# Feed-forward blocks 2 to 4 of a diffusion trunk: four tile pairs with a late 1/rms, eighteen with a normed operand

## The chip, the core and the metric

The kernel runs on one core of a Trainium2 chip. TensorE (PE) multiplies a stationary tile of 128 by 128 (PEld loads it) with a moving operand and writes into PSUM; VectorE (DVE) and ScalarE (ACT) work on tiles of 128 partitions; GpSimd (POOL) and SyncE (SP) issue transfers here. The metric is the device time of one execution in microseconds (us), the median of three.

## The reference

Two layers of a diffusion trunk over 256 latent tokens and 256 context tokens, width 1024. Each layer is a half-step feed-forward, token mixing, and a second half-step feed-forward. The context is needed only up to the first layer's mixing, so the first feed-forward block has 512 columns and the other three have 256. What the change touches is this:

```
def rms_norm(x, g):
    y = xf * lax.rsqrt(jnp.mean(xf * xf, axis=-1, keepdims=True) + EPS)
    return y * g
def modulate(x, g, shift, scale):
    return rms_norm(x, g) * (1 + scale) + shift
def swiglu(h, w13, w2):
    a, b = jnp.split(h @ w13, 2, axis=-1)        # 1024 -> 2 x 2816
    return (jax.nn.silu(a) * b) @ w2
def half_ffn(x, g, shift, scale, gate, w13, w2):
    return x + 0.5 * gate * swiglu(modulate(x, g, shift, scale), w13, w2)
```

## The kernel before

Activations lie with features on the partitions and tokens along the free dimension: X holds 8 parts (k = 0 to 7) of 128 features. Every product is made from split numbers: a float32 operand becomes a rounded high half (a CAST on ACT, L153) and the remainder (a subtraction on DVE, L154), and `mm3` issues three matmuls per part of the contraction: low weight by high operand (L148), high by high (L149), high weight by low operand (L150).

A feed-forward block first makes 22 pairs of tiles, f = 0 to 21 (one tile for `a`, one for `b`). A pair takes 2 tiles by 8 parts by 3 matmuls, 48 in all, of w13. `load_w` brings the pair's weights (raw, 2 buffers, issued by SP) and splits them in two halves of 1024 columns into whi and wlo (3 buffers each). `glu` then makes silu(a) * b and splits it into HH and HL. After pairs 0 to 10, and again after 11 to 21, eight products with w2 (33 matmuls each) are added to X.

In blocks 2 to 4 (`ffn` called with fi = 1, 2, 3 and n = T = 256) the norm is deferred. While the products before them still run, `prep_raw` writes the operand gs * x into AH and AL, columns 0 to 255, and `prep_shift` writes the shift into columns 256 and 257. The product is 258 columns wide, so that its last columns hold the shift's share. 1/rms is known later: `rstd` (L172 to L174: a matmul, a square root, a reciprocal into rb) is called after the first pair's products. `glu` multiplies each product with rb and adds the shift's column. The same columns 258 to 513 of AH and AL hold other operands in the mixers, where `prep_full` writes a fully normed operand for part of `mixer_c` (L192 to L194), and where `out_proj` reads its operand OH and OL, 256 columns wide.

Each engine works through its own list of instructions in order and waits on semaphores; a scheduler sets the order in each list when the kernel is built. In the trace block 2 runs its pairs from 504 us, block 3 from 695 us, block 4 from 959 us.

Of the kernel before, what the change touches and what calls it, by code (L numbers as in the profile page):

```python
# [29 lines left out]
# columns of the parameter table and of the constant table  # L30
# [5 lines left out]
def trunk(ctx: ExitStack, tc: tile.TileContext, I, out):  # L36
# [20 lines left out]
    # streams: 0 latent in layer 0, 1 context in layer 0, 2 latent in layer 1  # L57
# [26 lines left out]
    def finish_mod(layer, j, n=1, ks=slice(0, NK)):  # L84
        """add the bias to rows j .. j + n - 1; a scale becomes g * (1 + scale), the gates of
        half steps are halved"""
        st = slice(2, 3) if layer else slice(0, 2 if j < 5 else 1)
        ns, nk = st.stop - st.start, ks.stop - ks.start
        m = mod.rearrange("p s (j k) -> p s j k", k=NK)[:, st, j:j + n, ks]
        b = par[:, C_BMOD + layer * NMOD:C_BMOD + (layer + 1) * NMOD]  # L90
        b = b.rearrange("p (j k) -> p j k", k=NK)[:, j:j + n, ks].unsqueeze(1)
        V.tensor_tensor(out=m, in0=m, in1=b.broadcast_to([P, ns, n, nk]), op=ALU.add)
        sub, kind = (j + n - 1) // 3, (j + n - 1) % 3
        last = m[:, :, n - 1]
        if kind == 1:
            g0 = C_NG + (layer * 3 + sub) * NK
            g = par[:, g0 + ks.start:g0 + ks.stop].unsqueeze(1).broadcast_to([P, ns, nk])
            V.scalar_tensor_tensor(out=gs[:, st, sub, ks], in0=last, scalar=1.0, in1=g,
                                   op0=ALU.add, op1=ALU.mult)
        if kind == 2:  # L100
            V.tensor_scalar(gate[:, st, sub, ks], last, 1.0 if j == 5 else 0.5, None, ALU.mult)
# [4 lines left out]
    def run_mods(share):  # L106
        """take up modulation jobs as VectorE has room for them"""
        room[0] += share
        while mod_jobs:
            layer, i = mod_jobs[0]  # L110
            cost = 2 if layer == 0 and i < 40 else 1
            if room[0] < cost:
                return
            room[0] -= cost
            mod_jobs.pop(0)
            use_mod(layer, i, load_mod(layer, i, nc.gpsimd), tc.keep_in_program_order)
            if i % 8 == 7:
                finish_mod(layer, i // 8)
# [15 lines left out]
    def in_tiles(hi, lo, mhs, offs, w, late=False):  # L134
        """output tiles mhs of a pair, on the operand columns from each of offs; late: the
        products with the last part of the operand come last"""
# [30 lines left out]
    def rstd():  # L167
        """1 / rms of the rows whose squares acc holds; the users call it after their first products"""
# [13 lines left out]
    def prep_raw(k, off, xs, g):  # L182
        """operand parts of gs * x; the factor 1/rms follows after the product"""
# [5 lines left out]
    def prep_full(k, off, xs, r, g, sh):  # L189
        """operand parts of x / rms * gs + shift"""  # L190
        h = tmp.tile([P, T], F32, name="hn", bufs=2)
        V.tensor_tensor(out=h, in0=xs, in1=r, op=ALU.mult)  # L192
        S.activation(out=h, in_=h, func=AF.Identity, scale=g, bias=sh)
        split(AH[:, k, off:off + T], AL[:, k, off:off + T], h)  # L194

# [19 lines left out]
    def ffn(fi, layer, sub, n, mods, after, started=()):  # L215
        """n = T: latent only; n = 2T: latent | context share the products"""
        defer = n == T
        with tc.tile_pool(name=f"ffn{fi}", bufs=1) as fp:
            HH = fp.tile([P, NH, 2 * T], F32R, name="HH")
            HL = fp.tile([P, NH, 2 * T], F32R, name="HL")  # L220
            for half in range(2):
                hc = half * T if n == T else 0
                for fl in range(NH):
# [3 lines left out]
                    else:  # L227
# [3 lines left out]
                        ps = in_tiles(hi, lo, (0, 1), (0,), T + 2 if defer else n, late=f == 0)  # L231
# [45 lines left out]
    def out_proj(src, srcs, layer, after, loaded=()):  # L277
        """x += gate * (srcs @ w)"""
# [19 lines left out]
    def mixer_a(after):  # L298
        with tc.tile_pool(name="mixa", bufs=1) as mp:
# [12 lines left out]
            # keys and values of one key group, zero on the other group's rows / columns  # L312
# [9 lines left out]
            # the context's half of X is free from here on  # L322
# [11 lines left out]
            def proj(pair, mh, dst, ps=None, part=0):  # L334
                """dst = projected tile / rms, returns the shift's column"""
# [8 lines left out]
            def rotate(z):  # L344
                """rotary embedding; both elements of a pair have the same angle"""
# [98 lines left out]
            # unit u: head t of key group 0 or t + 4 of group 1, one block of 128 queries  # L444
# [177 lines left out]
    # ---- the first tiles, contraction outermost: each part of the modulation is used as it comes  # L622
    def start():
        ng = 4
        order = (0, 5, 1, 6, 2, 7, 3, 4)
        with tc.tile_pool(name="start", bufs=1) as sp:
# [14 lines left out]
            # brings the square root's table in while the squares are still to come  # L641
            S.activation(out=rb[:, 0:1], in_=cT[:, 0, 0:1], func=AF.Sqrt, scale=0.0, bias=epsb)
            # the vectors, on every partition
# [31 lines left out]
            def by_rows():  # L675
                """shift and scale of the last two parts, with the vectors as stationary operand"""
# [67 lines left out]
def _pack(x, c, ctx, c_ctx, w_mod, b_mod, norm_g, ffn_w13, ffn_w2, w_in_a, qk_norm_g, pool_w,  # L744
# [37 lines left out]
    # constants of the shapes alone  # L782
# [40 lines left out]
```

## Time and profile before

| | us |
|---|---|
| runs, median (lowest to highest) | 1156.89 (1154.97 to 1157.5) |
| span of the profiled execution | 1153.2 |
| PE busy in the span | 1143.4 (99%) |
| PEld busy | 1050.5 (91%) |
| DVE busy | 877.1 (76%) |
| ACT busy | 527.6 (46%) |

The page gives no time for the profiled execution beside its span. The span lies 3.7 us under the median of the runs; that is the time around it that the profile does not show. A matmul's own duration in the profile overlaps the next ones, so what a matmul costs is read from start to start.

### The profile page before, as it was taken

The numbers are of one execution on the slowest core, as the hardware profiler recorded it, in microseconds if no ns is written. First come the engines' busy times: TensorE is split into PE (matmuls) and PEld (weight loads), VectorE is DVE, ScalarE is ACT, GpSimd is POOL, SyncE is SP. The second block draws the span as 40 slices with busy tenths as digits, with TensorE's granted clock in tenths as the row PEclk, the third lists the DMA queues.
The fourth block names the chain that finished last, engine by engine and source line by source line (L and its number), as shares of the span: only waits on it lengthen the run. The fifth ranks groups of instructions, "written<-read, shape, count | busy, mean of one in ns | idle before, by whom it ended". The sixth has DMA issues, their size and how long they took to land.

```text
span 1153.2 us, 19338 instructions
## 1 busy us (share of the span) xinstructions
PE 1143.4 (99%) x7752; PEld 1050.5 (91%) x7752; DVE 877.1 (76%) x1614; ACT 527.6 (46%) x834; POOL 71.7 (6%) x148
## 2 busy tenths in 40 slices
PE   8999999999999999999999999999999999999998
PEld 4888888888888898999999999999999899999998
DVE  5968787878789988778778888756767788766763
ACT  5552212232223367665334456434445867434442
POOL 0000110212122200000010000000000000000000
PEclk9999999999999999999999999999999999999999
DMA  8835556788898930446587655446547535546543
GB/s 328 306 138 173 179 191 223 290 305 322 290 305 290 319 136 11 182 166 223 179 311 261 228 204 204 176 151 224 182 147 243 179 141 206 186 152 213 190 147 117
DMA packets 52410, 242.74 MB, mean 211 GB/s; under 512 B 5600, under 2 KB 11488, under 8 KB 38880
## 3 DMA queue, kind: packets, MB, share of 16 engines
q1 hardware_dynamic: 33888, 174.39, 42.6%
q0 software_dynamic: 18432, 67.12, 17.2%
q8 instruction: 61, 1.00, 0.4%
q14 instruction: 29, 0.24, 0.1%
HBM read 240.44 MB, written 1.05 MB: 209 GB/s over the span
## 4 chain that ended last, share of the span: by engine, by line
PE 98%; DVE 1%; ACT 1%; DMA 0%; issue 0%; SPq 0%
PE ps L150 31%; PE ps L148 31%; PE ps L149 31%; PE ps L473 1%; PE ps L681 1%; PE ps L602 1%; PE ps L603 1%; PE ps L601 1%; PE ps L664 1%; PE ps L649 0%; DVE wlo L154 0%; PE ps L172 0%; PE ps L350 0%; DMA ident<-in_ident 0%; PE ps L351 0%; DVE st L455 0%
## 5 line engine op out<-in xcount | busy, mean ns | idle before, releaser
L148 PE MATMUL ps<-AH,wlo 128*128 128x258 f32 (+2 forms) x1664 | 507.2, 305 | 0.3 <-ACT AH L153 0.3
L149 PE MATMUL ps<-AH,whi 128*128 128x258 f32 (+2 forms) x1664 | 506.6, 305 | 0.0
L150 PE MATMUL ps<-AL,whi 128*128 128x258 f32 (+2 forms) x1664 | 505.4, 305 | 0.0
L153 ACT CAST whi<-raw 128x1024 fp32r<-128x1024 f32 (+2 forms) x354 | 313.7, 921 | 362.4 <-PE ps L150 261.8
L154 DVE TENSOR_TENSOR wlo<-raw,whi 128x1024 fp32r<-128x1024 f32 (+2 forms) x354 | 367.6, 1064 | 54.8 <-ACT whi L153 53.7
L148 PEld LDWEIGHTS ps<-AH,wlo 128*128 128x128 f32 x1664 | 316.3, 190 | 15.3 <-PE ps L150 0.5
L149 PEld LDWEIGHTS ps<-AH,whi 128*128 128x128 f32 x1664 | 314.3, 189 | 14.8 <-issue 0.5
L150 PEld LDWEIGHTS ps<-AL,whi 128*128 128x128 f32 x1664 | 313.4, 189 | 14.2 <-DVE AL L154 0.2
L150 PE MATMUL ps<-HL,whi 128*128 128x256 f32 (+1 forms) x704 | 218.0, 310 | 0.0
L149 PE MATMUL ps<-HH,whi 128*128 128x256 f32 (+1 forms) x704 | 218.0, 310 | 0.0
L148 PE MATMUL ps<-HH,wlo 128*128 128x256 f32 (+1 forms) x704 | 218.0, 310 | 0.0
L80 DVE CUSTOM_DVE_ANT_0 wm<-wm,cc 128x1024 f32<-128x1024 f32 x138 | 164.8, 1220 | 5.1 <-DMA wm<-in_w_mod 4.5
L150 PEld LDWEIGHTS ps<-HL,whi 128*128 128x128 f32 x704 | 132.5, 188 | 7.8
L149 PEld LDWEIGHTS ps<-HH,whi 128*128 128x128 f32 x704 | 132.6, 188 | 7.7
L148 PEld LDWEIGHTS ps<-HH,wlo 128*128 128x128 f32 x704 | 132.5, 188 | 7.7
L72 POOL DMA_DIRECT2D wm<-in_w_mod x128 | 68.0, 531 | 560.5 <-DVE mod L80 506.6
L206 ACT ACTIVATE sa<-sa,cb 128x256 f32<-128x256 f32 x66 | 33.6, 510 | 120.7 <-DVE sa L205 117.5
L246 DVE SCALAR_TENSOR_TENSOR X<-ps,gate,X 128x256 f32<-128x256 f32 x64 | 30.9, 482 | 47.2 <-PE ps L150 47.2
L204 DVE COPY cb<-ps 128x1 f32<-128x1 f32 x66 | 10.3, 156 | 70.6 <-PE ps L150 70.5
L212 DVE TENSOR_TENSOR h<-ps,sa 128x512 f32<-128x512 f32 x22 | 15.2, 692 | 43.7 <-PE ps L150 34.6
L80 DVE CUSTOM_DVE_ANT_0 junk<-wm,cc 128x1024 bf16<-128x1024 f32 x34 | 41.5, 1219 | 8.6 <-ACT cc L651 7.7
L154 DVE TENSOR_TENSOR HL<-h,HH 128x256 fp32r<-128x256 f32 (+1 forms) x88 | 42.4, 486 | 0.0
(175 smaller groups left out, 793.2 us busy)
## 6 DMA issues: line engine op xcount, KB each, us to landing
raw<-in_w SPq DMA_DIRECT2D x84, 1024.0 KB, 4.9
wm<-in_w_mod POOLq DMA_DIRECT2D x128, 512.0 KB, 4.9
raw<-in_w SPq DMA_DIRECT2D x64, 704.0 KB, 4.1
wm<-in_w_mod SPq DMA_DIRECT2D x10, 512.0 KB, 7.0
raw<-in_w_in_a SPq DMA_DIRECT2D x5, 1024.0 KB, 7.5
raw<-in_w SPq DMA_DIRECT2D x8, 512.0 KB, 5.3
raw<-in_w_out_a SPq DMA_DIRECT2D x4, 1024.0 KB, 4.9
raw<-in_w_in_cu SPq DMA_DIRECT2D x4, 1024.0 KB, 4.9
```

Source lines behind the costliest of these rows:

```text
L72: eng.dma_start(out=w, in_=I["w_mod"][layer, i])
L80: pin(V.tensor_tensor_reduce(out=res, in0=w, in1=cc[:, st, :], scale=1.0, scalar=0.0, op0=ALU.mult, op1=ALU.add, accum_out=mod[:, 2 * laye ...
L148: PE.matmul(ps, wl, xh, start=first, stop=False)
L149: PE.matmul(ps, wh, xh, start=False, stop=False)
L150: PE.matmul(ps, wh, xl, start=False, stop=last)
L153: S.copy(hi, src)
L154: pin(V.tensor_tensor(out=lo, in0=src, in1=hi.bitcast(F32), op=ALU.subtract))
L206: S.activation(out=sa[:, :T], in_=sa[:, :T], func=AF.Silu, bias=cb[:, 0:1])
L212: V.tensor_tensor(out=h32[:, :n], in0=ps[1][:, :n], in1=sa[:, :n], op=ALU.mult)
L246: V.scalar_tensor_tensor(out=X[:, m, :T], in0=ps[:, :T], scalar=gate[:, 2 * layer, sub, m:m + 1], in1=X[:, m, :T], op0=ALU.mult, op1=ALU.add)
L473: PE.matmul(ps[:, i * P:i * P + P], pe[:, i * P:i * P + P], dg, start=True, stop=True)
L601: PE.matmul(ps[b], AL[:, k, ts], hi[:, ws], start=(k == 0), stop=False)
```

## The change

Blocks 2 to 4 keep the deferred form for pairs 0 to 3 only. Before the products of pairs 1, 2 and 3, the normed operand is made by `prep_full`, three parts, three parts and two (`FULL`), in columns 258 to 513 of AH and AL. Pairs 4 to 21 read that operand, 256 columns wide, and their `glu` takes the branch that before only block 1 took: SiLU straight from PSUM and one multiplication. Comments are also taken out.

```
+    NRAW, FULL = 4, (0, 3, 6, NK)
...
     def ffn(fi, layer, sub, n, mods, after, started=()):
-        """n = T: latent only; n = 2T: latent | context share the products"""
-        defer = n == T
+
+
+        raw, defer = n == T, False
...
-                        ps = in_tiles(hi, lo, (0, 1), (0,), T + 2 if defer else n, late=f == 0)
+                        if raw and 0 < f < NRAW:
+                            for k in range(*FULL[f - 1:f + 1]):
+                                prep_full(k, T + 2, X[:, k, :T], rb[:, :T],
+                                          gs[:, 2 * layer, sub, k:k + 1],
+                                          mod[:, 2 * layer, 3 * sub * NK + k:3 * sub * NK + k + 1])
+                        defer = raw and f < NRAW
+                        ps = in_tiles(hi, lo, (0, 1), (T + 2 if raw and not defer else 0,),
+                                      T + 2 if defer else n, late=f == 0)
```

VectorE's list in block 3, before, from the first product of pair 3 to the first of pair 4 (cb is the shift's column, sa and hn the two products times 1/rms, h the result, HL its low half; wlo are the low halves of later weights):

```order
L203 COPY cb<-ps 128x1
L205 TENSOR_TENSOR sa<-ps,rb 128x256
L204 COPY cb<-ps 128x1
L207 TENSOR_TENSOR hn<-ps,rb 128x256
L208 SCALAR_TENSOR_TENSOR h_6820<-hn,cb,sa 128x256
L154 TENSOR_TENSOR wlo<-raw,whi 128x1024 x2
L154 TENSOR_TENSOR HL<-h_6820,HH 128x256
```

The same place now, up to the low half of part 6 (hn<-X is prep_full's multiplication, AL<-hn the low half of a normed part; L205, L207, L209 and L210 are the old L203, L205, L207 and L208):

```order
L205 COPY cb<-ps 128x1
L207 TENSOR_TENSOR sa<-ps,rb 128x256
L192 TENSOR_TENSOR hn<-X,rb 128x256
L154 TENSOR_TENSOR wlo<-raw,whi 128x1024
L154 TENSOR_TENSOR AL<-hn,AH 128x256 x2
L209 TENSOR_TENSOR hn<-ps,rb 128x256
L192 TENSOR_TENSOR hn<-X,rb 128x256
L210 SCALAR_TENSOR_TENSOR h_6712<-hn,cb,sa 128x256
L206 COPY cb<-ps 128x1
L154 TENSOR_TENSOR wlo<-raw,whi 128x1024
L154 TENSOR_TENSOR HL<-h_6712,HH 128x256
L154 TENSOR_TENSOR AL<-hn,AH 128x256
```

Three of the eight parts still lie between pair 3's instructions, and a weight split, which reads what ScalarE cast, stands ahead of part 6's low half. Pair 2's result comes where pair 3's came before.

TensorE's list in block 3 at pair 4, before (ps_6839 is its first tile, ps_6840 its second; parts in order, first tile complete ahead of the second):

```order
L148 MATMUL ps_6839<-AH_72,wlo_6833 128x258
L149 MATMUL ps_6839<-AH_72,whi_6832 128x258
L150 MATMUL ps_6839<-AL_73,whi_6832 128x258
L148 MATMUL ps_6840<-AH_72,wlo_6833 128x258
L149 MATMUL ps_6840<-AH_72,whi_6832 128x258
```

The same place now (ps_6811 is the first tile of pair 4, ps_6812 the second; the piece begins 24 matmuls into the pair, where the first tile has had its parts 0 to 5):

```order
L148 MATMUL ps_6812<-AH_72,wlo_6805 128x256
L148 MATMUL ps_6811<-AH_72,wlo_6805 128x256
L149 MATMUL ps_6811<-AH_72,whi_6804 128x256
L149 MATMUL ps_6812<-AH_72,whi_6804 128x256
L150 MATMUL ps_6812<-AL_73,whi_6804 128x256
L148 MATMUL ps_6812<-AH_72,wlo_6805 128x256
L149 MATMUL ps_6812<-AH_72,whi_6804 128x256
L150 MATMUL ps_6812<-AL_73,whi_6804 128x256
L148 MATMUL ps_6812<-AH_72,wlo_6805 128x256
L150 MATMUL ps_6811<-AL_73,whi_6804 128x256
```

The two tiles are interleaved. Six parts of the first tile (18 matmuls) and seven matmuls of the second stand ahead of the first use of AH's part 6, and 33 matmuls ahead of AL's part 6; part 7 follows after 48 and 55 matmuls, six and nine of which belong to pair 5. In block 2 the uses of part 6 stand after 30 and 37 matmuls and the last of part 7 after 40; in block 4 after 39 and 43, and 46.

Outside pairs 4 to 21 of the three blocks TensorE's list is the same as before. So are SP's and POOL's lists throughout.

## Rows read from the trace of the kernel before

**Rows 1.** Page: busy time by engine, and the chain that ended last.
```profile
PE 1143.4 (99%) x7752; PEld 1050.5 (91%) x7752; DVE 877.1 (76%) x1614; ACT 527.6 (46%) x834; POOL 71.7 (6%) x148
...
PE 98%; DVE 1%; ACT 1%; DMA 0%; issue 0%; SPq 0%
```
**Rows 2.** Page: TensorE's granted clock in 40 slices, 9 is 90% or more.
```profile
PEclk9999999999999999999999999999999999999999
```
**Rows 3.** Timeline of TensorE, block 2: start us, duration us, line, out<-in.
```profile
599.78 0.28 PE L148 MATMUL ps<-AH,wlo 128*128 128x258 f32 x1
...
663.57 0.28 PE L148 MATMUL ps<-HH,wlo 128*128 128x256 f32 x1
...
694.89 0.28 PE L148 MATMUL ps<-AH,wlo 128*128 128x258 f32 x1
```
**Rows 4.** Timeline of TensorE in the first mixer's output projection.
```profile
487.74 0.28 PE L148 MATMUL ps<-AH,wlo 128*128 128x256 f32 x1
...
502.11 0.28 PE L148 MATMUL ps<-AH,wlo 128*128 128x256 f32 x1
```
**Rows 5.** Groups by line and form: busy us, mean ns | idle before, releaser.
```profile
L192 DVE TENSOR_TENSOR hn<-X,rb 128x256 f32<-128x256 f32 x8 | 3.0, 419 | 0.0
```
**Rows 6.** Timeline of VectorE: in block 2, in block 3, in block 4.
```profile
513.09 1.75 DVE L174 RECIPROCAL rb<-rb 128x256 f32<-128x256 f32 x1 [0.56 <-ACT rb L173]
...
519.35 0.16 DVE L203 COPY cb<-ps 128x1 f32<-128x1 f32 x1 [1.18 <-PE ps L150]
...
703.88 1.23 DVE L154 TENSOR_TENSOR wlo<-raw,whi 128x1024 fp32r<-128x1024 f32 x1 [1.22 <-ACT whi L153]
705.67 1.75 DVE L174 RECIPROCAL rb<-rb 128x256 f32<-128x256 f32 x1 [0.57 <-ACT rb L173]
707.34 0.10 DVE L203 COPY cb<-ps 128x1 f32<-128x1 f32 x1
...
708.48 0.42 DVE L205 TENSOR_TENSOR sa<-ps,rb 128x256 f32<-128x256 f32 x1
708.82 0.41 DVE L207 TENSOR_TENSOR hn<-ps,rb 128x256 f32<-128x256 f32 x1
709.15 0.15 DVE L204 COPY cb<-ps 128x1 f32<-128x1 f32 x1
709.21 0.41 DVE L205 TENSOR_TENSOR sa<-ps,rb 128x256 f32<-128x256 f32 x1
...
709.88 1.22 DVE L154 TENSOR_TENSOR wlo<-raw,whi 128x1024 fp32r<-128x1024 f32 x1
711.01 0.48 DVE L208 SCALAR_TENSOR_TENSOR h<-hn,cb,sa 128x256 f32<-128x256 f32 x1
711.40 0.15 DVE L203 COPY cb<-ps 128x1 f32<-128x1 f32 x1
...
966.09 1.75 DVE L174 RECIPROCAL rb<-rb 128x256 f32<-128x256 f32 x1 [0.24 <-ACT rb L173]
```
**Rows 7.** Timeline of ScalarE: a weight cast, and the second mixer's normed operand.
```profile
702.79 1.05 ACT L153 CAST whi<-raw 128x1024 fp32r<-128x1024 f32 x1 [1.71 <-DMA raw<-in_w]
...
898.34 1.08 ACT L193 ACTIVATE hn<-hn,mod,gs 128x256 f32<-128x256 f32 x2
899.32 0.70 ACT L153 CAST AH<-hn 128x256 fp32r<-128x256 f32 x2
899.92 0.91 ACT L569 ACTIVATE U<-z,cb 128x256 f32<-128x256 f32 x2
```
**Rows 8.** Timeline of TensorE: start of pair 4 in blocks 2, 3 and 4.
```profile
527.85 0.28 PE L148 MATMUL ps<-AH,wlo 128*128 128x258 f32 x1
...
718.50 0.28 PE L148 MATMUL ps<-AH,wlo 128*128 128x258 f32 x1
...
982.68 0.28 PE L148 MATMUL ps<-AH,wlo 128*128 128x258 f32 x1
```
**Rows 9.** Page: the transfers of w13's weights, us from issue to landing.
```profile
raw<-in_w SPq DMA_DIRECT2D x84, 1024.0 KB, 4.9
```

## The prediction

> **What bounds the kernel now.** I read the page first: the chain that ended last is 98% TensorE, and TensorE is busy 99% of the span; VectorE is idle for a quarter of the span and ScalarE for over half [rows 1]. The granted clock stands at its upper level, 2.4 GHz, in every slice [rows 2]. So nothing is won by giving VectorE less to do; the time changes only if a matmul gets cheaper or if TensorE has to wait. Since a matmul's duration overlaps the next, I took its price from the timeline, start to start. The 528 matmuls of pairs 11 to 21 of block 2, 258 columns wide, take 663.57 - 599.78 = 63.79 us, 120.81 ns each; the 264 of w2 behind them, 256 wide, take 31.32 us, 118.64 ns each [rows 3]. Block 2's two stretches follow each other without a gap.
>
> The first mixer's output projection is the nearest likeness of the new form: the same columns 258 to 513 of AH and AL, 256 wide, weights split and laid out by the same code, groups of 24. Its 120 matmuls between the two rows take 14.37 us, 119.75 ns each [rows 4].
>
> **What the change does.** *Narrower products.* In each block 18 pairs by 48 matmuls are 256 wide in place of 258: 3 x 864 = 2592. By the output projection each becomes 120.81 - 119.75 = 1.06 ns cheaper [rows 3, 4], in sum 2.75 us. The ends: nothing, if the width does not count in these stretches, and 120.81 - 118.64 = 2.17 ns, in sum 5.6 us, if they run as the w2 products do. I take 2.75, because the output projection shares operand, offset and group length, and w2's products share none of these.
>
> The Trainium skill (TensorE: Matmul & The Clock Gate, section Back-to-back issue gap) gives an isolated matmul N / 2.4 + 2.5 ns: two columns would be worth 0.83 ns, an estimate of 2.2 us in place of 2.75. The rows do not follow its level (109 ns for 256 columns against 119.75), so the row decides.
>
> *Less work in glu, more for the operand.* A pair in the old form costs VectorE two copies, two multiplications, one combined step and the low half; in the new form one multiplication and the low half. By starts in a row, a 256-wide step holds VectorE 0.335 us ((709.15 - 708.48) / 2), a copy 0.06, the combined step 0.39, a half weight split 1.13, the reciprocal 1.67 [rows 6]. So 54 pairs free 54 x (2 x 0.06 + 0.335 + 0.39) = 46 us, and 24 normed parts cost 24 x 2 x 0.335 = 16 us. ScalarE gains 24 x (0.49 + 0.30) = 19 us of work [rows 7]. None of it lies on the chain of waits; I cost it at nothing, hidden by TensorE's pairs of 48 x 120.81 ns = 5.80 us. The cover is thin in one place only: pairs 1 to 3, where both the old form and the normed parts must be done, and behind them pair 4, whose matmuls need all eight parts.
>
> *The new wait, block 3.* From the reciprocal at 705.67 the new list of VectorE has, ahead of part 6's multiplication, the reciprocal, 5 copies, 4 half splits, 2 combined steps and 21 steps of 256: 1.67 + 0.30 + 4.52 + 0.78 + 7.04 = 14.31 us, so that multiplication starts at 719.98, if nothing in the list waits. It takes 0.42 [rows 5], ScalarE's scaling 0.59 and its cast 0.40 (1.08 for two, the second 0.49 behind; 0.70, 0.30 behind) [rows 7], and a hand-over 0.04 (702.79 + 1.05 to 703.88) [rows 6, 7], three times: AH's part 6 is there at 721.51. Pair 4 starts at 718.50 [rows 8] and reads it after 25 matmuls of 119.75 ns, at 721.49. Just in time. AL's part 6 stands behind the multiplication (0.335) and 0.39 + 0.06 + 1.13 + 0.335 more, starts at 722.23, and is there 0.46 later, at 722.69; TensorE wants it after 33 matmuls, at 722.45: 0.24 late. AL's part 7 has a multiplication, another one, a half split and a combined step between: there at 725.22, wanted after 55, at 725.09: 0.13 late, less than the delay already taken. The list also waits for ScalarE here and there: part 1's low half has only 4 x 0.335 = 1.34 us of steps since its multiplication, and the way through ScalarE takes 1.53. I put 0 to 0.6 us on these waits and take 0.5. Block 3 then loses 0.24 to 0.84, say 0.7 us.
>
> *Blocks 2 and 4.* The same addition for block 2: 14.70 us from 513.09 are 527.79; VectorE reaches the copy of pair 2's first product after 4.99 us, at 518.08, and must wait until 519.35 for TensorE [rows 6], so 529.06. ScalarE scales parts 6 and 7 before it casts either: AH's part 6 at 530.94, wanted after 30 matmuls from 527.85, at 531.44 [rows 8]; AL's at 531.72, wanted after 37, at 532.28. Half a microsecond ahead, about what the waits may take: 0.1 us. In block 4 the list has 17.02 us from 966.09 [rows 6], to 983.11; AL's part 6 then comes at 985.7 and is wanted after 43 from 982.68, at 987.83 [rows 8]: two ahead, 0.1 us for more waits than I can see. What is queued behind a late part on VectorE are pair 3's and pair 4's results; they free PSUM banks, of which the kernel has eight, two to a pair, so that TensorE asks for pair 3's again with pair 7, 17 us on. The next pairs' weights (pair 5, at 5.75 us behind pair 4) are split in the same lists ahead of or beside parts 6 and 7, so nothing is late after that.
>
> *The rest.* `prep_shift` of the next norm no longer waits for pair 21; VectorE was not the bound there. Elsewhere TensorE's list and the transfers' are unchanged.
>
> **Sum.** -2.75 + 0.7 + 0.1 + 0.1 = -1.85 us: span 1153.2 to 1151.35 us. The runs lie 3.7 us above the span; their median 1156.89 becomes 1155.0, 0.16% lower. About 0.2%, 2.3 us, is what a measurement of this kernel can tell from no change.
>
> **The rivals.**
> - *No stall.* The scheduler's interleaving of pair 4 hides the late parts whole: -2.75 us, 1154.1 us. For it: blocks 2 and 4 come out ahead. Against it: block 3's low half of part 6 is late even with no wait counted.
> - *Width does not count.* If something other than the moving columns sets the spacing, the gain is nothing and the stalls of 0.9 stay: 1157.8 us. For it: PEld is busy 91% [rows 1], and 120 ns is above what 258 columns at 2.4 GHz (107.5 ns) would need. Against it: the 256-wide rows are cheaper in two places [rows 3, 4]. The Trainium skill (the same section) says that in a stream both the weight load and the matmul set the spacing, which would make this case likelier than the rows do.
> - *The rate of w2's products.* 118.64 ns: -5.6 + 0.9 = -4.7 us, 1152.2 us. Against it stands the output projection [rows 4].
> - *Slower: a weight load ahead of the last part.* In VectorE's list a weight split stands ahead of AL's parts 6 and 7, and in order. It needs ScalarE's cast, which needs the raw weights; their load starts when VectorE has read the buffer two pairs before and takes 4.9 us [rows 9]. That reading now comes later, since the normed parts stand before it. By the list, pair 6's load starts in block 3 after 10.1 us and the waits, at 715.8 to 716.4, and lands at 720.7 to 721.3; its split is due at 723.2 and the cast 1.05 before. From a landing 1 us later on, the split and with it AL's part 7 hold TensorE, microsecond for microsecond. Block 2 has pair 5's split and block 4 pair 6's in such a place. Two microseconds in each block would be 6 us: -2.75 + 0.9 + 6 = +4.2 us, 1161.0 us. It is slower by over 0.2% when the three blocks together lose more than 5.1 us.
> - *It does not do what it says:* the lists show the 256-wide matmuls and the normed parts, so I give this no chance.
>
> **Chances and range.** My forecast 0.52, no stall 0.17, the w2 rate 0.10, width does not count 0.08, slower 0.13. Faster by over 0.2%: no stall, the w2 rate and 0.08 of the forecast's own spread (stalls under 0.44), 0.35. Within 0.2%: 0.44 and 0.08, 0.52. Slower: 0.13. The forecast's own range, stalls from 0.24 to 2.2 us, is 1154.4 to 1156.4. For 8 in 10 I go down to 1152.8, most of the way to the w2 rate, and up to 1158.9, past the case without a gain and into mild forms of the slower one.
>
> **What would show it.** In the changed kernel's timeline the 256-wide matmuls of pairs 5 to 21 should be 119.7 to 119.8 ns apart, and a stretch of 528 (pairs 11 to 21) take 63.2 us in place of 63.79. TensorE should show one gap of 0.5 to 1 us inside pair 4 of block 3, on AH or AL's part 6, and none over 0.2 us in blocks 2 and 4. VectorE should hold 30 us less work (46 - 16) without any effect. A spacing of 120.8 or 118.7 ns makes the first term wrong; gaps of a microsecond or more at pair 4 in all three blocks, released by VectorE, make the second one wrong.

## The result and the profile after

The changed kernel is 0.2% slower: 1158.21 us against 1156.58 us for the kernel before on the same chip (medians of 18 runs each); the ratio of the means is 1.0020, 95% interval 1.0012 to 1.0029. Forecast were 1155.0 us and a gain of 0.16%.

One thing is needed to read the spans: in some executions the granted clock falls to 0.50 for some 2 us in the first mixer, which the change does not touch, and that costs 1.5 us; the profile of the changed kernel (run 1160.6 us, span 1158.8 us) is one of these, that of before is not, and what follows is counted from block 2's pair 1 on. The span is 5.6 us longer: 2.2 us up to there, where the change does nothing, 1.8 us from there to the last matmul, and 1.6 us behind it.

The page after, busy time and the chain that ended last, beside [rows 1]:

```profile
PE 1144.7 (99%) x7752; PEld 1050.2 (91%) x7752; DVE 843.2 (73%) x1446; ACT 540.4 (47%) x882; POOL 71.4 (6%) x148
...
PE 92%; DVE 3%; DMA 2%; ACT 2%; issue 0%; SPq 0%; ACTq 0%
```

VectorE works 34 us less, and yet DVE, DMA and ACT have come onto the chain, which TensorE held to 98%. The view of TensorE's waits (line, what it waited for: us in total, times, longest) says where. From block 2 on, before:

```profile
PE ps L148 <- ACT AH L153: 0.3, 1, 0.3
```

and after:

```profile
PE ps L611 <- DVE AL L154: 1.6, 1, 1.6
PE ps L148 <- ACT AH L153: 1.3, 3, 0.7
...
PE ps L150 <- DVE AL L185: 0.4, 1, 0.4
```

TensorE's timeline: block 2's pairs 11 to 21 begin, its w2 products begin, block 3's pair 0 begins (the answers to [rows 3]) and stops once; block 3's pair 4 begins (answer to [rows 8]) and stops twice.

```profile
601.82 0.28 PE L148 MATMUL ps<-AH,wlo 128*128 128x256 f32 x1
...
665.01 0.28 PE L148 MATMUL ps<-HH,wlo 128*128 128x256 f32 x1
...
696.33 0.28 PE L148 MATMUL ps<-AH,wlo 128*128 128x258 f32 x1
...
699.30 0.39 PE L150 MATMUL ps<-AL,whi 128*128 128x258 f32 x1 [0.40 <-DVE AL L185]
...
720.64 0.28 PE L148 MATMUL ps<-AH,wlo 128*128 128x256 f32 x1
...
722.52 0.39 PE L148 MATMUL ps<-AH,wlo 128*128 128x256 f32 x1 [0.27 <-ACT AH L153]
...
725.28 0.39 PE L148 MATMUL ps<-AH,wlo 128*128 128x256 f32 x1 [0.73 <-ACT AH L153]
```

The narrow products came as forecast: 665.01 - 601.82 = 63.19 us for 528, 119.7 ns each. Start to start, in us:

| stretch | before | after |
|---|---|---|
| pairs 11 to 21, each of three blocks | 63.79 | 63.19 |
| block 2, pairs 1 to 10 | 58.19 | 58.03 |
| block 3, pair 0 to pair 1 | 6.02 | 6.73 |
| block 3, pairs 1 to 10 | 58.19 | 59.69 |
| last mixer, v product | 22.34 | 24.22 |
| block 4, pairs 1 to 10 | 58.19 | 57.89 |

The differences add up to +1.8 us. The 2592 products give back 1.13 ns each, 2.9 us. Against that, 1.9 us are lost in block 3's pair 4, 0.7 us in its pair 0 and 1.9 us in the v product, and 0.3 us in pairs 4 of blocks 2 and 4. In pair 0 and in the v product the lists of all engines are the same as before.

### The profile page after: what moved, and what is told of

Same layout as the page of the kernel before. It is cut to its first block, busy times and chain, and to the rows that moved or that the text cites. A ratio compares the mean times of both kernels' runs of the same rounds, so it can differ in the third digit from the quotient of the medians.

```text
span 1158.8 us, 19125 instructions
## 1 busy us (share of the span) xinstructions
PE 1144.7 (99%) x7752; PEld 1050.2 (91%) x7752; DVE 843.2 (73%) x1446; ACT 540.4 (47%) x882; POOL 71.4 (6%) x148
## 4 chain that ended last, share of the span: by engine, by line
PE 92%; DVE 3%; DMA 2%; ACT 2%; issue 0%; SPq 0%; ACTq 0%
PE ps L148 29%; PE ps L150 29%; PE ps L149 29%; DVE wlo L154 2%; PE ps L483 1%; PE ps L691 1%; DMA raw<-in_w_in_cv 1%; ACT whi L153 1%; PE ps L674 1%; PE ps L612 1%; PE ps L613 1%; PE ps L611 1%; DMA raw<-in_w_in_cu 1%; PE ps L659 1%; DMA raw<-in_w 0%
## 5 line engine op out<-in xcount | busy, mean ns | idle before, releaser
L153 ACT CAST whi<-raw 128x1024 fp32r<-128x1024 f32 (+2 forms) x354 | 318.8, 921 | 429.5 <-PE ps L150 297.3
L148 PE MATMUL ps<-AH,wlo 128*128 128x256 f32 (+2 forms) x1664 | 506.2, 305 | 1.3 <-ACT AH L153 1.3
L149 PE MATMUL ps<-AH,whi 128*128 128x256 f32 (+2 forms) x1664 | 504.9, 304 | 0.0
L150 PE MATMUL ps<-AL,whi 128*128 128x256 f32 (+2 forms) x1664 | 503.5, 304 | 0.4 <-DVE AL L185 0.4
L154 DVE TENSOR_TENSOR wlo<-raw,whi 128x1024 fp32r<-128x1024 f32 (+2 forms) x354 | 372.2, 1065 | 93.2 <-ACT whi L153 92.5
L80 DVE CUSTOM_DVE_ANT_0 wm<-wm,cc 128x1024 f32<-128x1024 f32 x138 | 165.1, 1220 | 7.5 <-DMA wm<-in_w_mod 6.3
L214 DVE TENSOR_TENSOR h<-ps,sa 128x256 f32<-128x256 f32 (+1 forms) x76 | 38.1, 501 | 122.2 <-PE ps L150 113.0
L213 ACT ACTIVATE sa<-ps 128x256 f32<-128x256 f32 (+1 forms) x76 | 33.8, 445 | 89.0 <-PE ps L150 88.7
L80 DVE CUSTOM_DVE_ANT_0 junk<-wm,cc 128x1024 bf16<-128x1024 f32 x34 | 41.4, 1219 | 8.5 <-ACT cc L661 7.6
L153 ACT CAST HH<-h 128x256 fp32r<-128x256 f32 (+1 forms) x88 | 39.9, 455 | 13.2 <-DVE h L214 10.5
```

The lines of the kernel that those rows point to most:

```text
L80: pin(V.tensor_tensor_reduce(out=res, in0=w, in1=cc[:, st, :], scale=1.0, scalar=0.0, op0=ALU.mult, op1=ALU.add, accum_out=mod[:, 2 * laye ...
L148: PE.matmul(ps, wl, xh, start=first, stop=False)
L149: PE.matmul(ps, wh, xh, start=False, stop=False)
L150: PE.matmul(ps, wh, xl, start=False, stop=last)
L153: S.copy(hi, src)
L154: pin(V.tensor_tensor(out=lo, in0=src, in1=hi.bitcast(F32), op=ALU.subtract))
```

## Experiments

Theory A: what the change delays costs the time (A1: only pair 4's wait for the normed parts; A2: the added work delays weights). Theory B: the gaps elsewhere come and go in either kernel. All kernels were timed against before; the table behind the last of them gives the numbers. (The expectations count 2.85 us for the products; 2.9 is right.)

**again**, the changed kernel unaltered. 

> The changed kernel unaltered. Its profile showed 63.19 us for the 528 narrow products of pairs 11 to 21 in each block (63.79 before), a stall of 1.9 us in pair 4 of block 3, 0.2 and 0.1 us in pairs 4 of blocks 2 and 4, 0.7 us at pair 0 of block 3 and 1.9 us in the last mixer's v product, where the lists of all engines are the same as before. Theory A (the gaps outside the pairs are the change's doing, by weights that come later): the same gaps again, each within 0.5 us, time 0.1 to 0.3% above before. Theory B (those gaps come and go from one execution to the next in either kernel, only pair 4 is the change's): pair 4 stalls by 1.9 us again, and the gaps at pair 0 and at the v product differ by over 1 us in sum from the first profile.

The gaps are there again, but not the same: pair 4 stalls by 1.9 us, the end of block 2 and pair 0 of block 3 lose 4.1 us (0.7 in the first profile), the v product 0.1 (1.9). Neither theory as put: the cause is there both times, with a size that varies.

**nraw6**, six deferred pairs.
```
-    NRAW, FULL = 4, (0, 3, 6, NK)
+    NRAW, FULL = 6, (0, 2, 4, 6, NK, NK)
```


> Six pairs stay in the deferred form in place of four, so 16 pairs of each block are narrow and the normed parts are made over pairs 1 to 3 in two each and one more pair (2, 2, 2, 2); pair 6 is the first that reads them. The gain is then 16/18 of 2.85 us, 2.5 us. Theory A1 (what the change costs is the stall of the first pair that reads the normed parts): no gap over 0.25 us in pair 6 of any block, and 1156.6 - 2.5 = about 1154.1 us, 0.998 of before. Theory A2 (the cost is VectorE's and ScalarE's added work, which delays weights elsewhere): that work is the same here, so the time stays within 0.1% of the changed kernel, 1157 to 1159 us. Theory B: as A1, with gaps elsewhere that come and go.

The stall is gone, as A1 has it, but of the 2.5 us expected the runs show 0.7 (0.9994, not clear of no change): in the profile block 2's end and block 3's pair 0 lose 2.4 us, the v product 1.4.

**wide**, two columns more from the same start.
```
-                                      T + 2 if defer else n, late=f == 0)
+                                      T + 2 if raw else n, late=f == 0)
```


> As the changed kernel, but the products of pairs 4 to 21 read 258 columns from column 258 on, two more than are used. If the two columns are the whole gain, pairs 11 to 21 take 63.8 us again (120.8 ns each) in place of 63.19, and the time is 2.6 to 2.9 us above the changed kernel's, some 1161 us; the stalls of pair 4 stay. If the spacing fell for another reason (the offset, the form of glu), it stays at 119.7 ns and the time is that of the changed kernel, 1158 us.

The first term's reason falls: 258 columns from column 258 take 119.74 ns, only 0.06 more than 256, and the time is the changed kernel's. What made a product cheaper is not its width.

**unused**, the normed parts made and read by nothing.
```
-                        defer = raw and f < NRAW
+                        defer = raw
```


> The normed parts are made as in the changed kernel, but no product reads them: all 22 pairs stay in the deferred form, 258 wide. So the gain is gone, and no product waits for a normed part, while VectorE and ScalarE have the added 16 and 19 us of work. Theory A1 and theory B (the cost lies in pair 4's wait for the normed parts): the time of before, 1156.6 us within 0.1%. Theory A2 (the added work delays weights): 1 to 3 us above before, with gaps in pairs 2 to 6 or at later products, released by ScalarE's or VectorE's weight parts.

No gap from block 2 on that the kernel before does not have, 1.0004: the added work alone costs nothing that shows, so A2 falls. What is left between this kernel and the changed one is the products' operand and the shorter steps behind them.

The new profiles showed a difference that I had not looked for. VectorE's timeline of the changed kernel in block 2, pairs 19 to 21 (wlo: low halves of a weight split, HL: of a pair's result; L214: the new multiplication; L80: a modulation step, one of the jobs that work out the shifts, scales and gates of later blocks, each with a transfer of 512 KB of its own):

```profile
646.95 1.23 DVE L154 TENSOR_TENSOR wlo<-raw,whi 128x1024 fp32r<-128x1024 f32 x1 [4.23 <-ACT whi L153]
648.09 0.42 DVE L154 TENSOR_TENSOR HL<-h,HH 128x256 fp32r<-128x256 f32 x1
648.42 1.22 DVE L80 CUSTOM_DVE_ANT_0 wm<-wm,cc 128x1024 f32<-128x1024 f32 x1
...
649.57 1.22 DVE L154 TENSOR_TENSOR wlo<-raw,whi 128x1024 fp32r<-128x1024 f32 x1
650.70 0.42 DVE L214 TENSOR_TENSOR h<-ps,sa 128x256 f32<-128x256 f32 x1
...
658.79 0.89 DVE L154 TENSOR_TENSOR wlo<-raw,whi 128x704 fp32r<-128x704 f32 x1
```

HL and a modulation step stand between the two halves of one weight split, 649.57 - 648.09 = 1.5 us, and hold its raw buffer, of which there are two. Before, both halves stand together (x2):

```profile
649.45 2.36 DVE L154 TENSOR_TENSOR wlo<-raw,whi 128x1024 fp32r<-128x1024 f32 x2 [0.45 <-ACT whi L153]
```

Theory O: this order makes the loads in block 2 late. Theory F: TensorE is simply earlier than the weights can be.

**off_old**, the old steps kept on the new operand; 1/rms is then applied twice in pairs 4 to 21.
```
-                                      T + 2 if defer else n, late=f == 0)
+                                      T + 2 if raw else n, late=f == 0)
...
-                    glu(ps, defer, n, HH[:, fl, hc:hc + n], HL[:, fl, hc:hc + n])
+                    glu(ps, raw, n, HH[:, fl, hc:hc + n], HL[:, fl, hc:hc + n])
```


> As the changed kernel, but pairs 4 to 21 of blocks 2 to 4 keep the old steps behind the product (two copies, two multiplications, the combined step; 1/rms is applied twice there), on products 258 wide from column 258. It tells two things. Spacing: if the column offset of the operand makes a product cheaper, pairs 11 to 21 take 63.2 us per block (119.7 ns each); if it is the shorter steps behind the product, 63.8 us (120.8 ns). Lead: in the changed kernel and its kin VectorE's list has the low half of a result, and in block 2 a modulation step, between the two halves of each weight split; here they stand behind both halves, as before. Theory O (this order holds the raw buffers longer, so that in block 2 the weights lose their lead and TensorE waits at the end of block 2 and in pair 0 of block 3): no gap over 0.2 us from block 2's pair 11 to block 3's pair 1, where the changed kernel had 0.7 and 4.1 us and the variants 2.4 and 2.7. Theory F (TensorE is 2 to 3 us earlier there, and the weights come no faster whatever the order): gaps of 1 to 3 us there again, if the products run at 119.7 ns. Pair 4 of block 3 stalls by 2 us or more in both.

VectorE's timeline at the same place:

```profile
651.91 0.49 DVE L210 SCALAR_TENSOR_TENSOR h<-hn,cb,sa 128x256 f32<-128x256 f32 x1
652.34 1.69 DVE L154 TENSOR_TENSOR wlo<-raw,whi 128x704 fp32r<-128x704 f32 x2
653.95 0.42 DVE L154 TENSOR_TENSOR HL<-h,HH 128x256 fp32r<-128x256 f32 x1
654.29 1.22 DVE L80 CUSTOM_DVE_ANT_0 wm<-wm,cc 128x1024 f32<-128x1024 f32 x1
...
655.50 0.41 DVE L207 TENSOR_TENSOR sa<-ps,rb 128x256 f32<-128x256 f32 x1
```

The halves stand together (x2). Call the time from the end of a weight split to the first product that reads it the time in hand: the first w2 weights are ready at 652.34 + 1.69 = 654.03 us for a product at 662.62, 8.6 us in hand; in the changed kernel at 658.79 + 0.89 for 665.01, 5.3 us. No gap at the end of block 2, in pair 0 or in the v product, with products as cheap (119.74 ns): 0.9984. Theory O holds here and F does not. The stall of 2 us or more that was expected in pair 4 was 0.4 us. With more steps for VectorE than the changed kernel, this one is faster than before.

The longer hold is not the whole of it. In the changed kernel the two raw buffers come free at uneven times, so that two loads start 3 us apart (639.14 and 642.13 us) and run side by side, and each takes longer. The w13 loads of block 2's pairs 18 to 21, from issue to landing (least, median, most, us), before and in the changed kernel:

```profile
DMA to landing us min/median/max: 4.7/4.8/5.1
```
```profile
DMA to landing us min/median/max: 6.3/6.4/7.0
```

In off_old, whose modulation jobs are the same, they take 4.7 to 5.1 us again.

**new_at0**, narrow products from column 0; pairs 4 to 21 then leave out 1/rms and the shift.
```
-                        ps = in_tiles(hi, lo, (0, 1), (T + 2 if raw and not defer else 0,),
+                        ps = in_tiles(hi, lo, (0, 1), (0,),
```


> As the changed kernel, but pairs 4 to 21 read columns 0 to 255, so the operand without 1/rms and shift, which these pairs then leave out; the normed parts are made and not read. Products are 256 wide at offset 0, with the short steps behind them. If the offset sets the spacing, pairs 11 to 21 take 63.7 us or more (120.6 to 120.8 ns each); if the width or the short steps set it, 63.2 us (119.7 ns). No stall in pair 4 in either case. Theory O: gaps of 1 to 4 us from the end of block 2 to pair 0 of block 3 whatever the spacing is. Theory F: such gaps only if the spacing is 119.7 ns.

62.62 us, 118.60 ns each: here the width does count (258 from column 0: 120.81), and the start column as well (256 from column 258: 119.68). The gap of pair 0 stays (1.6 us).

**late_mods**, nraw6 with block 2's pairs free of modulation jobs.
```
-    ffn(1, 0, 2, T, (0.5, 1), next_norm(1, 0, T))
+    ffn(1, 0, 2, T, (0, 1), next_norm(1, 0, T))
```


> As the version with six deferred pairs (nraw6), but block 2's pairs take no modulation jobs; ten of them move into the first half of block 3. Theory O: without the modulation step between the halves of a split, and without its 512 KB transfers, the weights' lead in block 2's pairs 11 to 21 grows to 7 us, as in blocks 3 and 4, in place of 1 to 3.5, the gaps at the end of block 2 and in pair 0 of block 3 (2.4 us in nraw6) are gone or under 0.3 us; block 3's first half has the jobs and a lead of 1 to 4 us in their place, and may show gaps at its first w2 stretch. Time 1.0 to 2.4 us under nraw6 if it does not. Theory F: gaps of over 1 us at the end of block 2 stay.

In the pairs the time in hand grows to 7.5 us, as expected, but the jobs now run in w2's products, where it falls from 8.4 to -0.7 us: pair 0 loses 1.2 us and the time does not fall. The experiment moved the cause along.

**whole6**, nraw6 with the weights of pairs 7 to 21 split in one piece each.
```
-    def load_w(src, n, pin=lambda ins: ins):
+    def load_w(src, n, pin=lambda ins: ins, parts=2):
...
-        for c in (slice(0, n // 2), slice(n // 2, n)):
+        for c in [slice(j * n // parts, (j + 1) * n // parts) for j in range(parts)]:
...
-                        hi, lo = load_w(I["w13"][fi, f], 2048)
+                        hi, lo = load_w(I["w13"][fi, f], 2048, parts=1 if raw and f > NRAW else 2)
```


> As nraw6, but the weights of pairs 7 to 21 of blocks 2 to 4 are cast and split in one piece each, so that nothing stands between two halves in VectorE's or ScalarE's list and a raw buffer is free again as early as the list allows, with the modulation jobs where they were. Theory O: the lead in block 2's second half grows by 1 to 3 us, the gaps at the end of block 2 and in pair 0 of block 3 fall from 2.4 us to under 0.7; time 1.5 to 2.5 us under nraw6, 0.997 to 0.998 of before. Theory F: the gaps stay within 0.5 us of nraw6's and so does the time.

Half right: 7.3 us in hand at w2, the gap of pair 0 down to 0.6 us; but a whole split is ready later (for pair 7 4.3 us behind the landing; the first half 2.4 us in nraw6), and TensorE now waits 1 us for weights themselves ahead of block 2's pair 7. No gain.

**after_m**, the changed kernel without modulation jobs in block 2's last w2 products.
```
-                    if n > T or half == 0 or m < 4:
+                    if n > T or half == 0:
```


> As the changed kernel, but block 2's second round of w2 products takes no modulation jobs; the five that are left run in block 3's first pairs and first w2 products. Theory O says that the weights come to these w2 products with 3.3 to 5.3 us in hand in place of 8.0, and that the modulation steps and their transfers there use up 5 to 6 us more, until TensorE waits. Without them the loss should be about 4 us: no gap over 0.3 us at the end of block 2 and in pair 0 of block 3 (0.7 and 4.1 us in the changed kernel's two profiles), weights of pair 0 in hand 2 us or more before their use, and the stall in pair 4 of block 3 down from 1.9 to about 1.2 us, since the reciprocal then comes earlier. Time 1.5 to 3 us under the changed kernel's, 0.999 to 1.000 of before. Theory F (TensorE is simply earlier than the weights can be): the gaps stay within 0.5 us of the changed kernel's and so does the time.

As theory O has it: no gap at the end of block 2 or in pair 0 of block 3, and pair 4's stall down from 1.9 to 0.35 us. 1.0000 (0.9988 to 1.0012) in place of 1.0020 (1.0012 to 1.0029). A 1.0 us gap in the v product stays. The profile is the shortest of its twelve runs (1153.6 to 1159.5 us), so other executions may well show more than it does.

**at260**, the normed operand two columns further.
```
-                                prep_full(k, T + 2, X[:, k, :T], rb[:, :T],
+                                prep_full(k, T + 4, X[:, k, :T], rb[:, :T],
...
-                        ps = in_tiles(hi, lo, (0, 1), (T + 2 if raw and not defer else 0,),
+                        ps = in_tiles(hi, lo, (0, 1), (T + 4 if raw and not defer else 0,),
```


> As the changed kernel, but the normed operand lies in columns 260 to 515 in place of 258 to 513. If the start column sets the spacing (256 wide from column 0: 118.60 ns; from 258: 119.68 ns; w2's operands from 0 and 256: 118.64 ns), pairs 11 to 21 take 62.6 us per block in place of 63.19, in all 2592 x 1.08 = 2.8 us less; if only column 0 is cheap, 63.19 again. The gaps at pair 4 of block 3, at the end of block 2 and in pair 0 of block 3 stay or grow by up to 1 us in sum, since TensorE comes earlier still and the weights do not. Time 1.5 to 2.8 us under the changed kernel's in the first case, the same in the second.

TensorE's timeline, pairs 11 to 21 of block 2:

```profile
601.04 0.28 PE L148 MATMUL ps<-AH,wlo 128*128 128x256 f32 x1
...
662.97 0.28 PE L148 MATMUL ps<-HH,wlo 128*128 128x256 f32 x1
```

61.93 us, 117.29 ns each, below column 0's 118.60, which I had not expected. 0.9970, with 3.6 us lost around block 2's end.

**six260m** and **five260m**, both repairs (column 260, and no jobs as in after_m) and six or five deferred pairs (`NRAW, FULL = 5, (0, 2, 4, 6, NK)`). 

> Six deferred pairs, normed operand from column 260, and no modulation jobs in block 2's second round of w2 products: all three repairs at once. Products: 16/18 x 5.7 = 5.0 us less than before, if column 260 is as cheap as column 0. Theory O: no gap over 0.3 us in pairs 4 to 10, at the end of block 2 or in pair 0 of block 3, so 4 to 5 us under before, ratio 0.9955 to 0.997. Theory F: 2 us or more of it come back as waits for weights, ratio 0.998 or above.

> As six260m with five deferred pairs: 17/18 x 5.7 = 5.3 us less in the products, 0.3 us more than six260m. The normed parts are made in pairs 1 to 4 and first read in pair 5, so that the last of them has one pair (5.8 us) less time: by the changed kernel's stall of 1.9 us with four pairs, none is expected here. Time within 0.5 us of six260m; a stall of over 0.4 us in pair 5 of block 3 would make it the slower one.

0.9949 and 0.9939: no stall in the first normed pair of either. Some 1.1 to 1.3 us are still lost in block 2's last w2 products.

**spread**, five260m with no modulation job in block 2's second half; blocks 3 and 4 take them.
```
-                    if f >= len(started) and (n > T or 3 <= f):
+                    if f >= len(started) and (n > T or 3 <= f) and not (fi == 1 and half):
...
-    ffn(2, 1, 0, T, (0.5, 1), next_norm(1, 1, T))
+    ffn(2, 1, 0, T, (0.25, 0), next_norm(1, 1, T))
```


> As five260m, but block 2's whole second half takes no modulation jobs; the ten that are left are spread over the pairs of blocks 3 (one in four pairs) and 4. By theory O the weights in block 2's second half then come to w2 with 7 us in hand in place of 2.9, and the gaps of 1.1 us in its first w2 products are gone; in block 3's pairs they have 3 us or more and no gap appears. Time 0.8 to 1.2 us under five260m. If gaps of 0.5 us or more appear in block 3 or 4 in their place, nothing is won.

TensorE's timeline, block 2's pairs 11, w2 and block 3's pair 0, and TensorE's waits from block 2 on:

```profile
598.61 0.28 PE L148 MATMUL ps<-AH,wlo 128*128 128x256 f32 x1
...
660.54 0.28 PE L148 MATMUL ps<-HH,wlo 128*128 128x256 f32 x1
...
691.86 0.28 PE L148 MATMUL ps<-AH,wlo 128*128 128x258 f32 x1
```
```profile
PE ps L611 <- DVE AL L154: 0.7, 1, 0.7
PE ps L148 <- ACT AH L153: 0.3, 1, 0.3
```

61.93 and 31.32 us, no gap up to the v product, and w2's first weights with 8.2 us in hand; 0.9936, the lowest ratio of the study. Against five260m the intervals overlap, so the 0.8 to 1.2 us expected in the time are not shown.

**shift5** and **shiftb**, 30 and 84 idle products at the head of the first mixer, in five260m and in before.
```
+            ps = bank()
+            for _ in range(30):
+                PE.matmul(ps[:, :2], AH[:, 0, :P], AH[:, 0, :2], start=True, stop=True)
```


> As five260m with 30 more products of two columns, of no use, at the start of the first mixer, so that TensorE's list is 60 instructions longer from there on and the 16 KB packets of the instruction queue (one for each 256 instructions of TensorE) come some 3.7 us earlier at every later place. In five260m they stand 0.9 and 20.1 us behind the first load of the last mixer's weights, beside the tails of the first and fourth load. Theory I (such a packet holds one of the 16 DMA engines and with it the last piece of a weight load): they move to about -3 and 16.5 us, where they stand in the profiles without a gap; the first load lands within 5.0 us (5.5 there), and the v product's gap of 0.9 us is gone or under 0.2. Theory C (chance, or the weights' lead): the gap stays within 0.4 us. Time: 30 x 0.06 = 2 us more for the products themselves, less the gap.

> As the kernel before, with 84 such products at the start of the first mixer: 168 instructions, by which the instruction packets come some 10 us earlier at every later place. Before they stand 0.6 us ahead of the mixer's first weight load and 15.2 us behind it; now about 5 us behind it. Theory I: the first load then lands later than 5.4 us (4.9 before), the fourth's cast later than 8.3 us behind its issue (7.6 before), and the v product shows a gap of 0.3 to 1.9 us, which the kernel before does not have. Theory C: no gap, since the lists and the weights' lead there are those of the kernel before. Time: about 5 us more for the products themselves.

In shift5 the v product's gap is gone and the first load is in within 4.9 us, as theory I has it. But the kernel is slower than five260m (0.9991 against 0.9939): in its profile the first mixer takes 5.1 us more where 2 were expected, and block 2's first half loses 3.2 us, most of it in w2's products and ahead of pair 11, to weights and results that come late; why they do is open. In shiftb the packet came 4.3 us behind that load, as planned, but the load was not later (cast 5.0 us behind its issue) and there is no gap. So the packet is not shown to be the cause. (The idle products cost 15 us there, not 5: the granted clock is 0.50 from 400 to 415 us, while they run and just behind them.)

The numbers: ratio to before with 95% interval; ns of one product in pairs 11 to 21 (width, first column); us lost at the end of block 2 and in pair 0 of block 3, in the first normed pair of block 3, and in the v product. The ratios are those of all runs; ns and losses come from one profile each, and again shows how far a loss can differ from one execution to the next.

| kernel | ratio | ns (form) | end of 2 | first normed | v |
|---|---|---|---|---|---|
| before | 1 | 120.81 (258, 0) | 0 | - | 0 |
| after | 1.0020 (1.0012 to 1.0029) | 119.68 (256, 258) | 0.7 | 1.9 | 1.9 |
| again | 1.0019 (1.0009 to 1.0029) | 119.68 | 4.1 | 1.9 | 0.1 |
| nraw6 | 0.9994 (0.9981 to 1.0007) | 119.68 | 2.4 | 0 | 1.4 |
| wide | 1.0019 (1.0007 to 1.0031) | 119.74 (258, 258) | 2.7 | 2.5 | 0 |
| unused | 1.0004 (0.9995 to 1.0013) | 120.81 (258, 0) | 0 | - | 0 |
| off_old | 0.9984 (0.9973 to 0.9996) | 119.74 (258, 258) | 0 | 0.4 | 0 |
| new_at0 | 0.9978 (0.9966 to 0.9991) | 118.60 (256, 0) | 1.6 | - | 0.8 |
| late_mods | 1.0005 (0.9994 to 1.0016) | 119.68 | 1.2 | 0 | 1.4 |
| whole6 | 1.0001 (0.9990 to 1.0011) | 119.7 | 0.6 | 0 | 0.1 |
| after_m | 1.0000 (0.9988 to 1.0012) | 119.68 | 0 | 0.35 | 1.0 |
| at260 | 0.9970 (0.9958 to 0.9982) | 117.29 (256, 260) | 3.6 | 1.9 | 0.6 |
| six260m | 0.9949 (0.9934 to 0.9963) | 117.29 | 1.3 | 0 | 0.4 |
| five260m | 0.9939 (0.9917 to 0.9961) | 117.29 | 1.1 | 0 | 0.8 |
| spread | 0.9936 (0.9923 to 0.9949) | 117.29 | 0 | 0 | 0.9 |
| shift5 | 0.9991 (0.9979 to 1.0003) | 117.29 | 0.8 | 0.2 | 0 |
| shiftb | one run, 1171.9 us | 120.81 (258, 0) | 0 | - | 0 |

## Why the prediction was wrong

**The step that failed** is the one on the steps behind the product: "None of it lies on the chain of waits; I cost it at nothing, hidden by TensorE's pairs of 48 x 120.81 ns = 5.80 us". I counted VectorE's work, which fell, and not what its list became. HL and the modulation step came to stand inside a weight split, 1.5 us, and the loads that this bunched took 1.6 us longer each. Off_old shows it by the one side (old steps: no loss at the end of block 2 or in pair 0), after_m and spread by the other (no modulation jobs there: no loss). With the new steps in blocks 3 and 4, which have no such jobs, the pairs keep 7.5 us in hand. Why the scheduler laid the list out so is not shown.

From block 2 on, -1.85 us were forecast and +1.8 came in the first profile, 3.7 us apart: 0.7 us in pair 0 and 1.2 of pair 4's 1.9 us are the late weights, 1.9 us are the v product, whose cause stays open. In the second profile it is 4.1, 1.2 and 0.1 us.

How a late load stops TensorE is seen in the changed kernel's second profile (again). VectorE's multiplication for the last pair's result, then ScalarE's timeline, the end of block 2 and pair 0 of block 3:

```profile
666.66 0.42 DVE L214 TENSOR_TENSOR h<-ps,sa 128x256 f32<-128x256 f32 x1 [1.39 <-PE ps L150]
...
670.69 0.78 ACT L153 CAST whi<-raw 128x704 fp32r<-128x704 f32 x1 [6.06 <-DMA raw<-in_w]
671.37 0.40 ACT L153 CAST HH<-h 128x256 fp32r<-128x256 f32 x1
...
701.37 1.05 ACT L153 CAST whi<-raw 128x1024 fp32r<-128x1024 f32 x1 [1.58 <-DMA raw<-in_w]
702.33 0.51 ACT L184 ACTIVATE AH<-X,gs 128x256 fp32r<-128x256 f32 x1
```
and TensorE's waits there:
```profile
PE ps L148 <- ACT HH L153: 1.7, 1, 1.7
...
PE ps L150 <- DVE AL L185: 0.7, 1, 0.7
```

TensorE waits not for the weights that are late, but for the last pair's result HH and for an operand part (AL, made from ScalarE's AH), which stand in ScalarE's list behind a cast that waits for a transfer. The Trainium skill (PSUM — Partial Sum Buffer, section Engine vs sequencer instructions) says that the queues of ScalarE and VectorE are strictly first in, first out; the rows agree: h was there at 666.66 + 0.42 = 667.08 us, and HH's cast starts at 671.37, right behind the weights' cast, which waited 6.06 us. Block 2's w2 products use up the rest in both kernels: from their start to block 3's pair 0 the time in hand falls from 8.0 to 1.8 us before and from 5.3 to -0.25 after (the first profile; the second half of a weight block is read later than the first). So before, the reserve sufficed.

**The gain: right size, wrong reason.** 1.06 ns were forecast and 1.13 came (2.9 us in place of 2.75). The output projection was the right likeness because it reads the same columns [rows 4], not because of its width. The prediction took it for its offset among other things, so the size is not luck alone; but it put the gain down to the two columns less, and that was wrong here. The start column sets the price: from 258 the width is worth 0.06 ns (wide), from 0 it is worth 2.21. The rival that width does not count was right for this column and wrong in its price of nothing. The w2 rate, "against it stands the output projection", was to be had at another column: 118.60 ns at 0, 117.29 at 260. The formula that the Trainium skill (TensorE: Matmul & The Clock Gate, section Back-to-back issue gap) gives for an isolated matmul has only the number of columns in it and so makes two columns worth the same 0.83 ns, an estimate, from every start; the streams here gave 0.06 and 2.21 ns, and they decide.

**The stall: right place, short by the same cause.** 0.7 us in block 3 were forecast, 1.9 came. VectorE kept the pace that was worked out: from its reciprocal to part 6's multiplication 14.98 us, against 14.31 and 0.5 for waits. But pair 4 began 720.64 - 708.53 = 12.11 us behind the reciprocal, not 718.50 - 705.67 = 12.83 [rows 6, 8]: the reciprocal waits for a square root on ScalarE that stands behind a weight cast, which comes 9.33 us behind pair 0's start (705.66 us) in place of 7.90 (702.79 [rows 7]), and an earlier part held TensorE as well (the stop at 722.52). Where the weights are on time, the stall is 0.35 (after_m) and 0.4 us (off_old), in the forecast's 0.24 to 0.84. Blocks 2 and 4 lost 0.2 and 0.1 us, where 0.1 each was forecast.

**The slower rival** named the mechanism, a weight load behind a raw buffer that is freed later, and looked for it at AL's last parts. It came instead where the reserve is smallest, behind block 2's w2 products, and cost 0.7 to 4.1 us, not 6.

**The base.** The 3.7 us between the span of before and the median of its runs are two things: a run lasts 1.8 us longer than its span (1160.6 and 1158.8 us in the changed kernel's profile), and by that the profiled execution of before, 1155.0 us, was 1.9 us shorter than the median. The forecast difference does not hang on it.

**"Elsewhere TensorE's list and the transfers' are unchanged"** is true of the lists and was taken for the times. The v product lost 0 to 1.9 us where nothing in the lists differs.

**What stays open** is that gap. Of 13 profiles with the new steps nine show 0.4 to 1.9 us, and of four with the old steps none. TensorE stops there for AL, an operand part made from ScalarE's AH, and AH stands in ScalarE's list behind the cast of the first v weights, which waits longer for its transfer; before and in the changed kernel:

```profile
894.21 2.00 ACT L153 CAST whi<-raw 128x1024 fp32r<-128x1024 f32 x2 [1.78 <-DMA raw<-in_w_in_cv]
```
```profile
900.17 2.00 ACT L153 CAST whi<-raw 128x1024 fp32r<-128x1024 f32 x2 [4.13 <-DMA raw<-in_w_in_cv]
```

That transfer takes, from issue to landing (last column, us), before and in the changed kernel:

```profile
raw<-in_w_in_cv SPq DMA_DIRECT2D x1, 1024.0 KB, 7.5
```
```profile
raw<-in_w_in_cv SPq DMA_DIRECT2D x1, 1024.0 KB, 9.3
```

In the 17 profiles it takes 6.8 to 8.7 us where the gap is 0.1 us or none, and 8.4 to 10.0 us where it is 0.4 us or more. What makes it long is not shown: an instruction packet beside the mixer's first load goes with the gap in most profiles, but shiftb had one 4.3 us behind that load and again one 4.5 us behind it (4.4 in the first profile, with its 1.9 us), and neither lost more than 0.1 us.

## What to carry to other kernels

A step that gets cheaper on an engine off the path changes the order of that engine's list: look in the new order at what now stands between the pieces of a step that frees a buffer, and behind an instruction that waits for a transfer; and look whether buffers that come free at uneven times make loads run side by side. Work out the weights' time in hand at the start and the end of each stretch with a shorter period, since a reserve that shrinks from 8 to 5 us shows only where the next stretch uses up more. And price a product by the start column of its operand as well as by its width: moving the operand two columns on, from 258 to 260, was worth 2.39 ns a product here, twice what the change itself gave.

## What the runs showed of the hardware

In a stream of weight load and product (fp32r, 128x128 weights, granted clock at 2.4 GHz) the spacing depends on where the moving operand starts in its row of 516 columns: 256 columns take 118.60 ns from column 0, 119.68 from 258 and 117.29 from 260; 258 columns take 120.81 from 0 and 119.74 from 258. Why, no run here tells.

In the first mixer TensorE waits 1.9 us for ScalarE in every profile. Behind that wait the granted clock falls to its lower level, 1.2 GHz, in 8 of the 15 profiles without idle products and stays at 2.4 GHz in seven, with the same matmuls in the mixer: in unused, which has the steps of before, it falls, and in off_old it stays. TensorE's windows of the changed kernel (us, busy, granted clock, DMA share, GB/s):

```profile
441.00:447.00 6.00, 4.12 (x21) 0.91 0.00 0
447.00:449.00 2.00, 2.00 (x7) 0.50 0.00 0
```

In the profile of before the same windows have 1.00. The mixer takes 1.5 to 1.6 us longer where the clock falls.
